# Thirty-two more bytes in two small tiles: starts of the large SBUF tiles in a decoder trunk

## The chip, the cores and the metric

The kernel runs on one core of one Trainium2 chip. The metric is the device time of one execution in microseconds (us); it is given as the median of the runs. A core has a matrix engine (PE, TensorE) that reads both operands from SBUF and adds into PSUM, a vector engine (DVE), an activation engine (ACT), GpSimd (POOL), a queue engine that issues loads (SP), and DMA engines. SBUF has 128 partitions; a tile takes the same byte range in each, and "start" below is the first byte of that range.

## The reference

A trunk of two layers over 256 tokens of width 2048, all in fp32, for one batch:

```python
for i in range(DEPTH):                       # DEPTH = 2
    h = rmsnorm(x, norm_mix[i])
    if i < N_A_LAYERS:                       # layer 0
        x = x + gmlp_mixer(h, ...)           # gelu(h @ w_in), spatial gate, @ w_out
    else:                                    # layer 1
        x = x + nsa_mixer(h, *kvs, ...)      # attention: compressed, selected, window
    x = x + swiglu(rmsnorm(x, norm_ffn[i]), ffn_w_in[i], ffn_w_out[i])   # 2048 -> 5632 -> 2048
    x = ple_add(x, p[i], norm_ple[i], ple_w[i], ple_gate[i])             # gated 2048 x 2048
    if i == N_A_LAYERS - 1:
        kvs = shared_kv(x, ...)              # K/V of three branches, block compression MLP
```

## The kernel before, in words

Every matrix product is made of three matmuls with fp32r operands (`mm3`, lines 101 to 104): each fp32 operand is split into a high and a low part (`split`, lines 92 to 99: ACT copies the high part, DVE subtracts it), and high by high, high by low and low by high are added in PSUM. The activations are the stationary operand (128 columns, loaded by LDWEIGHTS), the weights the moving one, 512 columns wide in most places: the pair of a weight load and a matmul of 512 columns is what the program mainly consists of.

The stages follow each other: the gMLP mixer's `v` and `u` (the input product), its output product `ao`, the FFN of layer 0 (`ffn_unit` makes one 512-column chunk of gate and up in products `p1` to `p7` by a Strassen-like scheme; `fo` is the output product), the gated embedding (`pj`, `pg`), the shared K/V and the attention (`kv`, `ph`, `q`, `s`, `pv`), its output product `bo`, and the FFN and the embedding of layer 1. Weights stream from HBM through `wraw` (line 139, issued on SP) into a tile `raw`, are split into `wh` and `wl`, and are used at once. `weave` (line 178) puts side work between the blocks of a product; nothing in the order depends on the addresses.

Tiles come from pools that lie one behind the other in SBUF in the order in which they are opened. `const` (line 67) holds `ident`, `pk` (gains and other constants, 197 floats a partition, line 77), `neg_half` and the residual stream `x_sb`. `actp` holds the stationary operands: `big_pair` (line 193) makes the pairs hA, hF, hP, hKV, hB under the tag "h" and gT, aT, oT under the tag "big". `tp` holds temporaries (t13 and t24 of the FFN, qh, ql), `sm` small ones (`ssk`, line 640, two buffers of 4 floats), then come the weight pools `w_raw`, `w_wh`, `w_wl` and, in the FFN stages, `w_third` and `exp` with the FFN's extra stationary forms exh and exl (`new_forms`, line 218). In the attention the pools `bp` (KTh, KTl, Vh, Vl) and `at` (pah, pal, pbh, pbl, L) lie there instead. A size is rounded up to 32 bytes, so a tile of 197 floats moves all that lies behind it off a multiple of 512.

Of the kernel before, what the change touches and what calls it, by code (L numbers as in the profile page):

```python
# [9 lines left out]
F32 = mybir.dt.float32  # L10
# [8 lines left out]
P = 128  # L19
# [27 lines left out]
PK_W = PK_ANY + 1  # L47
# [16 lines left out]
def trunk_kernel(ctx: ExitStack, tc: tile.TileContext, a: dict, out: bass.AP):  # L64
    nc = tc.nc

    const = ctx.enter_context(tc.tile_pool(name="const", bufs=1))
    act_p = ctx.enter_context(tc.tile_pool(name="actp", bufs=1))
    tp = ctx.enter_context(tc.tile_pool(name="tp", bufs=2))
    sm = ctx.enter_context(tc.tile_pool(name="sm", bufs=2))  # L70
# [3 lines left out]

    ident = const.tile([P, P], F32, name="ident")
    make_identity(nc, ident)
    pk = const.tile([P, PK_W], F32, name="pk")
    nc.scalar.dma_start(pk, a["pk"])
    neg_half = const.tile([P, 16], F32, name="neg_half")
    nc.vector.memset(neg_half, -0.5)  # L80
    x_sb = const.tile([P, TT, D], F32, name="x_sb")
# [10 lines left out]
    def split(hi, lo, src, scale=None):  # L92

        if scale is None:
            nc.scalar.activation(hi, src, AF.Copy)  # L95
            nc.vector.tensor_tensor(lo, src, f32v(hi), ALU.subtract)  # L96
        else:
            nc.scalar.activation(hi, src, AF.Copy, scale=scale)
            nc.vector.scalar_tensor_tensor(lo, src, scale, f32v(hi), op0=ALU.mult, op1=ALU.subtract)
# [25 lines left out]
    def gen_bank(nm):  # L125
        return ps_gen.tile([P, NC], F32, tag="gen", name=nm)

    def rsqrt_mean(dst, ss, n):

        w = ss.shape[-1]  # L130
        ms = sm.tile([P, 16], F32, tag="ms", name="ms")
        pr = ss.shape[0]
        nc.vector.tensor_scalar(ms[:pr, :w], ss, 1.0 / n, EPS, op0=ALU.mult, op1=ALU.add)
        nc.gpsimd.tensor_tensor(dst, ms[:pr, :w], neg_half[:pr, :w], ALU.pow)
# [409 lines left out]
    with ExitStack() as bctx:  # L544
# [85 lines left out]
        def kv_proc(br, accs):  # L630
            kr = tp.tile([P, TT, G, HD], F32, tag="t0", name="kr")
            for t in range(TT):
                r1 = rs[:, t:t + 1]
                nc.scalar.activation(kr[:, t].rearrange("p g d -> p (g d)"), accs[t][:, :256], AF.Copy, scale=r1)
                split(Vh[:, br, t].rearrange("p g d -> p (g d)"), Vl[:, br, t].rearrange("p g d -> p (g d)"),
                      accs[t][:, 256:], r1)
            sq = tp.tile([P, TT * G, HD], F32, tag="t2", name="sqk")
            krf = kr.rearrange("p t g d -> p (t g) d")
            nc.scalar.activation(sq, krf, AF.Square)
            ssk = sm.tile([P, 4], F32, tag="ssk", name="ssk")  # L640
            nc.vector.tensor_reduce(ssk, sq, axis=AX.X, op=ALU.add)
            rk = sm.tile([P, 4], F32, tag="rk", name="rk")
            rsqrt_mean(rk, ssk, HD)
            nc.vector.tensor_tensor(krf, krf, rk.unsqueeze(2).to_broadcast([P, 4, HD]), ALU.mult)

            def k_T():
                pt = gen_bank("ksT")
                for g in range(G):
                    for t in range(TT):
                        nc.tensor.transpose(pt[:, g * SEQ + t * P:g * SEQ + (t + 1) * P], kr[:, t, g, :], ident)  # L650
                for t in range(TT):
                    bs = slice(16 + t * 256 + br * P, 16 + t * 256 + (br + 1) * P)
                    split(KTh[:, :, bs], KTl[:, :, bs], pt.rearrange("p (g t s) -> p g t s", g=G, t=TT)[:, :, t],
                          pk[:, PK_KN + 1 + br:PK_KN + 2 + br])
            return k_T
# [28 lines left out]

        accs = gemm("kv0", kvT[0], kvT[1], a["kv_w"], CH_D, NC, KD)
        k_T = kv_proc(0, accs)
        hT = big_pair("h", "hB")
        side = [rest, k_T] + [lambda c=c: x_chunk_T(hT, G_MIX1, c) for c in range(NCH)]
        accs = gemm("kv1", kvT[0], kvT[1], a["kv_w"], 2 * CH_D, NC, KD, side)
        k_T = kv_proc(1, accs)  # L690
        accs = gemm("kvc", kvT[0], kvT[1], a["kv_w"], 0, NC, KD, [rest, rest, k_T, rest])
        c_T = cmp_proc(accs)
# [294 lines left out]
```

## Time and profile before

| | us |
|---|---|
| median of three runs | 2329.65 |
| lowest and highest | 2329.06, 2333.55 |
| the profiled execution | 2328.34 |
| its span, from first to last instruction | 2326.6 |

| engine | busy us | share of the span |
|---|---|---|
| PE (matmul) | 2301.5 | 99% |
| PEld (weight loads, beside the matmuls) | 1871.1 | 80% |
| DVE | 1596.1 | 69% |
| ACT | 1170.5 | 50% |
| POOL | 26.6 | 1% |

The rows further down come from one profiled execution. A row of the timeline is one instruction with its start and its duration. Matmuls overlap in the array and their ends are modelled, so the distance between two starts tells the pace, the duration doesn't. In names like `p<-wh,hF0h` the result stands first, then the moving and the stationary operand; buffer numbers are left out.

### The profile page before, as it was taken

The numbers are of one execution on the slowest core, as the hardware profiler recorded it, in microseconds if no ns is written. First come the engines' busy times: TensorE is split into PE (matmuls) and PEld (weight loads), VectorE is DVE, ScalarE is ACT, GpSimd is POOL, SyncE is SP. The second block draws the span as 40 slices with busy tenths as digits, with TensorE's granted clock in tenths as the row PEclk, the third lists the DMA queues.
The fourth block names the chain that finished last, engine by engine and source line by source line (L and its number), as shares of the span: only waits on it lengthen the run. The fifth ranks groups of instructions, "written<-read, shape, count | busy, mean of one in ns | idle before, by whom it ended". The sixth has DMA issues, their size and how long they took to land.

```text
span 2326.6 us, 26376 instructions
## 1 busy us (share of the span) xinstructions
PE 2301.5 (99%) x10419; PEld 1871.1 (80%) x10419; DVE 1596.1 (69%) x1783; ACT 1170.5 (50%) x1335; POOL 26.6 (1%) x26
## 2 busy tenths in 40 slices
PE   8999999999999999999999999999999999999999
PEld 6887788888888888877787987888888888888887
DVE  5565588855887478655567776688747886588544
ACT  6554455533554345445457665555434554355443
POOL 0000000000000000000000000000000000000000
PEclk9999999999999999999999999999999999999999
DMA  8665655565555555555557444455555455455553
GB/s 293 186 188 192 216 215 199 181 206 180 193 199 199 186 193 179 201 186 175 170 177 228 118 143 145 163 199 199 199 182 198 173 207 199 164 207 200 184 191 127
DMA packets 117720, 438.53 MB, mean 188 GB/s; under 512 B 8555, under 2 KB 10731, under 8 KB 117084
## 3 DMA queue, kind: packets, MB, share of 16 engines
q1 hardware_dynamic: 116220, 434.38, 54.1%
q10 hardware_dynamic: 1296, 2.20, 0.3%
q8 instruction: 82, 1.34, 0.2%
q0 software_dynamic: 80, 0.26, 0.0%
q14 instruction: 42, 0.34, 0.0%
HBM read 434.68 MB, written 6.46 MB: 190 GB/s over the span
## 4 chain that ended last, share of the span: by engine, by line
PE 94%; DVE 2%; DMA 2%; ACT 1%; issue 1%; POOL 0%; SPq 0%; DVEq 0%; ACTq 0%
PE p L103 13%; PE p L104 13%; PE p L102 13%; PE fo L102 7%; PE fo L104 7%; PE fo L103 7%; PE pg L104 3%; PE pg L102 3%; PE pg L103 3%; PE ao L103 1%; PE u L102 1%; PE u L104 1%; PE u L103 1%; PE ao L104 1%; PE ao L102 1%; PE bo L103 1%
## 5 line engine op out<-in xcount | busy, mean ns | idle before, releaser
L96 DVE TENSOR_TENSOR wl<-raw,wh 128x2048 fp32r<-128x2048 f32 (+4 forms) x486 | 891.0, 1841 | 575.5 <-ACT wh L95 574.7
L95 ACT ACTIVATE wh<-raw 128x2048 fp32r<-128x2048 f32 (+4 forms) x486 | 754.8, 1555 | 779.8 <-PE fo L104 275.5
L95 ACT ACTIVATE wh<-t 128x1024 fp32r<-128x1024 f32 x132 | 134.6, 1054 | 168.4 <-PE p L104 118.4
L103 PE MATMUL p<-wl,hF1h 128*128 128x512 f32 x462 | 183.5, 397 | 0.0
L103 PE MATMUL p<-wl,hF0h 128*128 128x512 f32 x462 | 183.5, 397 | 0.0
L102 PE MATMUL p<-wh,hF1h 128*128 128x512 f32 x462 | 182.6, 395 | 0.0
L102 PE MATMUL p<-wh,hF0h 128*128 128x512 f32 x462 | 182.6, 395 | 0.0
L104 PE MATMUL p<-wh,hF1l 128*128 128x512 f32 x462 | 182.6, 395 | 0.0
L104 PE MATMUL p<-wh,hF0l 128*128 128x512 f32 x462 | 182.6, 395 | 0.0
L96 DVE TENSOR_TENSOR wl<-t,wh 128x1024 fp32r<-128x1024 f32 x132 | 157.1, 1221 | 15.7 <-ACT wh L95 13.8
L104 PE MATMUL p<-wh,exl 128*128 128x512 f32 x418 | 164.4, 393 | 0.0
L103 PE MATMUL p<-wl,exh 128*128 128x512 f32 x418 | 164.1, 393 | 0.0
L102 PE MATMUL p<-wh,exh 128*128 128x512 f32 x418 | 163.6, 391 | 0.0
L104 PEld LDWEIGHTS p<-wh,hF1l 128*128 128x128 f32 x462 | 86.8, 188 | 20.5
L102 PEld LDWEIGHTS p<-wh,hF1h 128*128 128x128 f32 x462 | 86.8, 188 | 20.6
L104 PEld LDWEIGHTS p<-wh,hF0l 128*128 128x128 f32 x462 | 86.8, 188 | 20.5
L102 PEld LDWEIGHTS p<-wh,hF0h 128*128 128x128 f32 x462 | 86.8, 188 | 20.6
L103 PEld LDWEIGHTS p<-wl,hF1h 128*128 128x128 f32 x462 | 86.8, 188 | 20.3
L103 PEld LDWEIGHTS p<-wl,hF0h 128*128 128x128 f32 x462 | 86.8, 188 | 20.3
L102 PE MATMUL fo<-wh,aT_0h 128*128 128x512 f32 x256 | 101.1, 395 | 0.0
L102 PE MATMUL fo<-wh,aT_1h 128*128 128x512 f32 x256 | 101.1, 395 | 0.0
L103 PE MATMUL fo<-wl,aT_0h 128*128 128x512 f32 x256 | 100.9, 394 | 0.0
(288 smaller groups left out, 4402.3 us busy)
## 6 DMA issues: line engine op xcount, KB each, us to landing
raw<-in_ffn_w_in SPq DMA_DIRECT2D x176, 1024.0 KB, 4.9
raw<-in_ffn_w_out SPq DMA_DIRECT2D x88, 1024.0 KB, 4.9
raw<-in_a_w_in SPq DMA_DIRECT2D x64, 512.0 KB, 3.8
raw<-in_ple_gate SPq DMA_DIRECT2D x32, 1024.0 KB, 4.9
raw<-in_a_w_out SPq DMA_DIRECT2D x16, 1024.0 KB, 4.9
raw<-in_kv_w SPq DMA_DIRECT2D x24, 512.0 KB, 4.0
raw<-in_b_w_out SPq DMA_DIRECT2D x10, 1024.0 KB, 4.9
raw<-in_b_w_in SPq DMA_DIRECT2D x24, 384.0 KB, 3.4
```

The costliest lines, as they stand in the source:

```text
L95: nc.scalar.activation(hi, src, AF.Copy)
L96: nc.vector.tensor_tensor(lo, src, f32v(hi), ALU.subtract)
L102: nc.tensor.matmul(ps, lh, rh, start=start, stop=False)
L103: nc.tensor.matmul(ps, lh, rl, start=False, stop=False)
L104: nc.tensor.matmul(ps, ll, rh, start=False, stop=stop)
```

## The change

Two small tiles get 32 bytes more a partition each: `pk` is allocated with 205 floats instead of 197 (the load fills the first 197), and the two buffers of `ssk` with 12 floats instead of 4 (the first 4 are used).

```diff
     ident = const.tile([P, P], F32, name="ident")
     make_identity(nc, ident)
-    pk = const.tile([P, PK_W], F32, name="pk")
-    nc.scalar.dma_start(pk, a["pk"])
+
+    pk = const.tile([P, PK_W + 8], F32, name="pk")
+    nc.scalar.dma_start(pk[:, :PK_W], a["pk"])
...
-            ssk = sm.tile([P, 4], F32, tag="ssk", name="ssk")
+            ssk = sm.tile([P, 12], F32, tag="ssk", name="ssk")[:, :4]
```

The built programs have the same instructions in the same order with the same waits on every engine. They differ in starts. This is what lies where, in bytes from the start of a partition, and in brackets the remainder by 512:

| tiles | before | after |
|---|---|---|
| x_sb | 17888 (480) | 17920 (0) |
| hA, hF, hP, hKV, hB, high part (`actp`) | 34272 (480) | 34304 (0) |
| gT, aT, oT, high part (`actp`) | 67040 (480) | 67072 (0) |
| t13, t24, qh, ql and others (`tp`) | 99808 to 120288 (480) | 99840 to 120320 (0) |
| raw, wh, wl (FFN stages) | 127904 to 193440 (416) | 128000 to 193536 (0) |
| exh, exl | 201632, 211360 (416) | 201728, 211456 (0) |
| T of the compression MLP (slices of 240 bytes) | 67040, 83424 (480) | 67072, 83456 (0) |
| KTh, KTl | 177056 (416), 181280 (32) | 177152 (0), 181376 (128) |
| Vh, Vl | 185504, 189600 (160) | 185600, 189696 (256) |
| L, two buffers | 203584 (320), 206784 (448) | 203680 (416), 206880 (32) |
| pbh, pbl, pah, pal | 210176 to 224512 (256) | 210272 to 224608 (352) |

The slices that a matmul reads start at whole multiples of 512 bytes into hA to hP, gT to oT, ex, wh and wl where a block is 512 or 384 columns wide, so the remainder holds for them as well.

## Rows read from the trace of the kernel before

**Rows 1.** The page: span, busy time by engine, the chain that ended last.

```profile
span 2326.6 us, 26376 instructions
PE 2301.5 (99%) x10419; PEld 1871.1 (80%) x10419; DVE 1596.1 (69%) x1783; ACT 1170.5 (50%) x1335; POOL 26.6 (1%) x26
...
PE 94%; DVE 2%; DMA 2%; ACT 1%; issue 1%; POOL 0%; SPq 0%; DVEq 0%; ACTq 0%
```

**Rows 2.** Stretches: us, then PE, PEld, DVE, ACT, POOL busy, PEclk, DMA share, GB/s.

```profile
389.62:433.03 43.41, 43.41 (x193) 35.20 (x192) 37.45 (x35) 22.89 (x20) 0.00 (x0) 1.00 0.54 194
500.00:600.00 100.00, 100.00 (x431) 80.37 (x430) 58.34 (x40) 41.05 (x26) 0.00 (x0) 1.00 0.52 181
1371.00:1446.00 75.00, 70.18 (x349) 57.22 (x349) 46.95 (x100) 40.92 (x93) 1.64 (x1) 0.95 0.37 129
```

**Rows 3.** Timeline of PE, FFN output stage: start us, us, engine, line, operation, shapes.

```profile
539.94 0.39 PE L102 MATMUL fo<-wh,aT_0h 128*128 128x512 f32 x1
...
546.94 0.39 PE L102 MATMUL fo<-wh,aT_0h 128*128 128x512 f32 x1
```

**Rows 4.** Timeline of PE at the end of attention.

```profile
1430.30 0.63 PE L103 MATMUL bo<-wl,oTh 128*128 128x512 f32 x1
...
1431.58 0.61 PE L104 MATMUL bo<-wh,oTl 128*128 128x512 f32 x1
```

**Rows 5.** ACT and DVE by shape: count, busy us, mean ns, idle before.

```profile
L95 ACT ACTIVATE wh<-raw 128x1024 fp32r<-128x1024 f32 x132 | 138.6, 1058 | 132.3 <-PE u L104 31.5 <-PE v L104 24.9 <-PE pg L104 22.2
L95 ACT ACTIVATE wh<-t 128x1024 fp32r<-128x1024 f32 x132 | 134.6, 1054 | 168.4 <-PE p L104 118.4 <-DVE t L445 47.2 <-DVE t L442 2.9
...
L95 ACT ACTIVATE pah<-pa 128x512 fp32r<-128x512 f32 x16 | 9.4, 586 | 5.4 <-PE pa L751 5.4
...
L95 ACT ACTIVATE aT_0h<-mT 128x512 fp32r<-128x512 f32 x16 | 8.5, 584 | 0.0
L96 DVE TENSOR_TENSOR wl<-raw,wh 128x1024 fp32r<-128x1024 f32 x132 | 160.8, 1223 | 119.7 <-ACT wh L95 119.3
L96 DVE TENSOR_TENSOR wl<-t,wh 128x1024 fp32r<-128x1024 f32 x132 | 157.1, 1221 | 15.7 <-ACT wh L95 13.8
```

**Rows 6.** Timeline of PE in an FFN unit: nine matmuls on ex tiles.

```profile
364.13 0.39 PE L102 MATMUL p<-wh,exh 128*128 128x512 f32 x1
...
365.52 0.39 PE L102 MATMUL p<-wh,exh 128*128 128x512 f32 x1
...
366.20 0.40 PE L102 MATMUL p<-wh,hF0h 128*128 128x512 f32 x1
366.44 0.39 PE L103 MATMUL p<-wl,hF0h 128*128 128x512 f32 x1
```

**Rows 7.** PE by shape: count, busy us, mean ns.

```profile
L103 PE MATMUL p<-wl,hF1h 128*128 128x512 f32 x462 | 183.5, 397 | 0.0
...
L104 PE MATMUL p<-wh,hF0l 128*128 128x512 f32 x462 | 182.6, 395 | 0.0
L104 PE MATMUL p<-wh,exl 128*128 128x512 f32 x418 | 164.4, 393 | 0.0
...
L102 PE MATMUL p<-wh,exh 128*128 128x512 f32 x418 | 163.6, 391 | 0.0
```

**Rows 8.** Timeline of PE in attention: 512 columns after 256, and values.

```profile
1250.22 0.61 PE L102 MATMUL q<-wh,hBh 128*128 128x512 f32 x2
1250.67 0.40 PE L103 MATMUL q<-wl,hBh 128*128 128x512 f32 x1
...
1284.33 0.28 PE L103 MATMUL pv<-pbl,Vh 128*128 128x256 f32 x1
...
1284.93 0.27 PE L751 MATMUL pa<-ident,L 128*128 128x128 f32 x1
```

**Rows 9.** Timeline of PE in the compression MLP: sixteen matmuls on T.

```profile
1223.89 0.28 PE L576 MATMUL ph<-wh,T 128*128 128x256 f32 x1
...
1225.78 0.35 PE L102 MATMUL q<-wh,hBh 128*128 128x432 f32 x1
```

## The prediction

> **What bounds the kernel now.** I read the page first: TensorE is busy over 99% of the span, and the chain of work that ended last lies on it for 94%; DVE has 2%, DMA 2%, ACT 1% [rows 1]. So anything this change does to copies, loads or activations can touch about 5% of 2326.6 us, and a change of the matmuls' own pace touches nearly all of it. Second, the windows by stretch: in one FFN unit (389.62 to 433.03) PE is busy all 43.41 us while DVE works 37.45 (86%), ACT 22.89, and in the FFN's output stage PE is busy 100 of 100 us and DVE 58 [rows 2]. PE sets the pace there, and the others have room of at least 14%.
>
> Third, the timeline of PE, read from start to start, since the ends of pipelined matmuls are modelled. In the FFN's output stage 30 matmuls of 512 columns start between 539.94 and 546.94 us: 233.3 ns each, at a granted clock of 1.00 [rows 2, 3], which is the 2.4 GHz level. 512 columns at one a cycle would be 213.3 ns. In the stretch whose granted clock averages 0.95 [rows 2] the same matmuls start 0.427 us apart, three in 1.28 [rows 4], and 512 columns at 1.2 GHz are 427 ns: there nothing is added to the columns. So 20 ns of each 233 do not belong to the array's column rate. They belong to something that feeds it, and that is where an address could matter.
>
> **Part 1: what the change removes, adds, moves.** No instruction is added or removed and none changes place on any engine; the copy of `pk` moves the same 197 columns. Only starts in SBUF move. By the built programs `const` and `actp` and `tp` tiles go from 480 to 0 (counted within 512 bytes) and the weight tiles raw, wh, wl and the ex tiles from 416 to 0; the attention's tiles do not reach multiples of 512 (pah, pal, pbh, pbl go from 256 to 352). So the words of the change hold for the operands of the large matmuls, not for the attention.
>
> **Part 2: DVE, ACT, DMA.** Before the change the same operation already stands on different starts. ACT's 128x1024 copy takes 1058 ns from raw (416 to 416) and 1054 ns from t13/t24 (480 to 416); DVE's subtraction behind it 1223 and 1221 ns; ACT's 128x512 from PSUM takes 586 ns into pah (256) and 584 into aT (480) [rows 5]. Three starts, 0.4% apart: I cost these at nothing. All of it lies beside PE anyway, and if it came to 0.4% of the chain's DVE and ACT 3%, it would be 0.3 us. For loads the trace has no second start: a partition gets 4096 bytes in a row, and a start off 512 can touch at most one more piece of 512, an eighth; of DMA's 2% of the chain (46 us) that is an estimated 6 us either way at most. With no row that shows any of it I take zero.
>
> **Part 3: the matmuls.** In the kernel before, the moving operand of a large matmul (wh, wl) starts at 416 and the stationary one (hA, hF, aT, gT, oT, hP, hKV, all in `actp`) at 480: 64 bytes apart. There is one exception, the FFN's ex tiles: stationary at 416, as the moving ones. And these are faster. In a run of nine of them the starts go from 364.13 to 366.20, 230 ns each, and the last three, 365.52 to 366.20, take 0.68 us, 226.7 each; the next operand from hF at 366.20 falls back to the old pace [rows 6]. By group the same is seen in the modelled durations: 391 and 393 ns for ex, 395 and 397 for hF of the same shape [rows 7]. The first six of the nine take 1.39 us, 232 each: the pace falls by and by, so short runs show only part of it. A second sight of the same floor: after 256-column matmuls two of 512 columns start at 1250.22 and the third start is 1250.67, 225 ns each [rows 8]. So 226 to 227 ns is a pace that PE reaches with these operands, and 233.3 one that it is held at in long runs of 416 against 480. What differs for ex is the start within 512 bytes (equal for both operands), and also the place (above byte 200,000, where the others lie below 100,000); the trace can't part these two. After the change both operands of all these matmuls start at 0, so they are equal as ex's are.
>
> Evidence against: 256-column matmuls show no dependence. Sixteen in a row on T, whose slices step by 240 bytes through eight different starts, take 1.89 us, 118 ns each; those on Vh with a moving operand at 256 start 0.60 us for five, 120 ns [rows 8, 9]. Neither is a long run of one relation at 512 columns, and that is where the loss is, so I let ex decide and keep the doubt as a rival.
>
> The sum: the groups by shape hold 8,969 matmuls of 512 columns, 1,254 of them on ex tiles, 418 in each of three groups [rows 7]. 141 of the others start after a wait or another kind and are left out: 7,574 on 416 against 480 at 233.3, and 1,254 on ex at about 230. At 226.5 (between 226.7 and 226) the first gain 6.8 ns, 51.5 us, and the second 3.5 ns, 4.4 us (in longer runs of one relation they would stay at their last pace). Some 2 us of the 56 fall in stretches in which PE waits anyway: 1371 to 1446, for one, has 4.8 of 75 us idle [rows 2]. 54 us are left. Is the room there? The FFN unit's 43.41 us would be about 42.3 with DVE at 37.45, 89%, so nothing else becomes late; and the loads keep the DMA engines busy for 0.52 to 0.54 of these stretches [rows 2]. The profiled execution's own 2328.34 us becomes 2274; the median of the runs shown, 2329.65, becomes 2275. I say 2274.
>
> The spread of this: pace between 225 and 228 ns gives 2262 to 2287.
>
> One rule speaks against all this. The Trainium skill, "SBUF — State Buffer", section "Who interferes with whom", gives TensorE two SBUF read ports, one for the moving operand and one for the weight load, independent of each other, and says that PE never waits on anyone; by it the relation of two starts is worth nothing, and the time stays at 2330. The ex rows [rows 6] speak against it, the 256-column rows [rows 9] for it.
>
> **Rivals.** *No change.* The ex tiles are faster for their place or for the work around them, not for their start, and 233.3 stays. For it: the flat 256-column rows, and that DVE, ACT and DMA are indifferent. Against: no row with 480 against 416 holds 227 over a run, and none of the tiles' other traits has a reason in the trace. The time is 2329.65 within 0.2% (4.7 us, about what a measurement here can tell from no change): 2325 to 2334.
>
> *Deeper.* If equal starts are half of the loss and the straddling of a 512-byte line the other half, aligned tiles go below what ex shows, towards the 213.3 ns of the columns; halfway, 220 ns, the sum is 8,828 times 12.8 ns (from the mean of 232.8 over both kinds), 113 us: 2217. For it: at the lower clock nothing is added to the columns [rows 4]. Against: the 225 to 227 of [rows 6, 8] look like a floor. The Trainium skill, "TensorE: Matmul & The Clock Gate", section "Back-to-back issue gap", gives N/2.4 + 2.5 ns, 215.7 for 512 columns; by that alone it would be an estimated 2179, and the trace disagrees before the change by 17.1 ns a matmul.
>
> *Slower.* Weight load and moving stream now begin at the same byte of a 512-byte row, always, and if two readers of one row get in each other's way, each matmul pays. It decides from 0.5 ns per matmul (4.7 us over 8,969). The upper bound is the largest single step among the rows at that pace, 0.24 us from 366.20 to 366.44 [rows 6]: 6.7 ns more, 59 us; half of it, an estimate, gives 2359. Against: ex has equal starts too and is faster.
>
> *In between.* Only part of the stages gains, as ex does in short runs (230 instead of 226.5): about 3 ns on 8,828, 27 us, 2303.
>
> **How the numbers follow.** The pace of 226.5: 0.40, 2274. In between: 0.08. Deeper: 0.11. No change: 0.30. Slower: 0.11. That is faster 0.59, same 0.30, slower 0.11. The range of 8 in 10 goes from 2225 (the upper half of the deeper case) to 2335 (the end of no change); it leaves out the slower case and about half of the deeper one. For the likeliest case alone it is 2262 to 2287.
>
> **What would show it.** In the profile after, the 30 matmuls of the output stage should take 6.8 us instead of 7.00, an FFN unit 42.3 instead of 43.41, and the ex and hF groups should have the same duration. If the pace is 233.3 still, the start is not the cause. If hF and ex differ as before, it is the place. If the start-to-start times fall and the span doesn't, another engine took over, and the idle time before PE names it. DVE and ACT durations should be within 0.5% of [rows 5]; if they moved, part 2 was wrong.

## The result, and the profile after

| | before | after |
|---|---|---|
| median, us | 2329.36 | 2277.57 |
| lowest and highest | 2326.11, 2333.55 | 2275.97, 2278.04 |
| span of the profiled execution | 2326.6 | 2275.6 |

The ratio of the times is 0.9775, with an interval of 0.9759 to 0.9792. The line of the copy of `pk` is one lower in the changed kernel, so L104 of [rows 7] is L105 here.

The page of the changed kernel: span, busy time by engine, and the chain that ended last.

```profile
span 2275.6 us, 26376 instructions
...
PE 2250.2 (99%) x10419; PEld 1873.7 (82%) x10419; DVE 1592.9 (70%) x1783; ACT 1170.0 (51%) x1335; POOL 26.6 (1%) x26
...
PE 94%; DVE 2%; DMA 2%; ACT 1%; issue 1%; POOL 0%; SPq 0%; DVEq 0%; ACTq 0%
```

PE's busy time fell by 51.3 us and the span by 51.0; PEld, DVE and ACT have the busy time that they had, within 0.2%, and the chain's shares are those of [rows 1]. So nothing came late in place of PE: the work is the same, and PE goes through it faster. The timeline of PE in the FFN's output stage, to be laid beside [rows 3], with 30 matmuls between the two starts:

```profile
523.01 0.39 PE L103 MATMUL fo<-wh,aT_0h 128*128 128x512 f32 x1
...
529.81 0.39 PE L103 MATMUL fo<-wh,aT_0h 128*128 128x512 f32 x1
```

6.80 us, 226.7 ns each, where it was 233.3. And the nine matmuls on ex tiles of [rows 6], with three on hF behind them:

```profile
355.77 0.39 PE L103 MATMUL p<-wh,exh 128*128 128x512 f32 x1
...
357.13 0.39 PE L103 MATMUL p<-wh,exh 128*128 128x512 f32 x1
...
357.81 0.39 PE L103 MATMUL p<-wh,hF0h 128*128 128x512 f32 x1
...
358.49 0.39 PE L103 MATMUL p<-wh,hF0h 128*128 128x512 f32 x1
```

The first six take 1.36 us (226.7 each), the last three 0.68 (226.7), and the three on hF 0.68 as well. The uneven first matmuls of an ex run are gone, and so is the step back up after it. Uneven they were, and not falling by and by: as means over the runs on ex before, the first seven steps from start to start are 229.7, 231.4, 230.1, 235.2, 229.2, 232.0 and 230.8 ns, and only the eighth and ninth are 226.6 and 226.7. After, all nine are 226.6 or 226.7. By shape (count, busy us, mean ns) the same product on hF and on ex now differs by 2 ns (391, 389), where [rows 7] have 395 and 397 for hF against 391 and 393 for ex:

```profile
L104 PE MATMUL p<-wl,hF1h 128*128 128x512 f32 x462 | 180.4, 391 | 0.0
...
L104 PE MATMUL p<-wl,exh 128*128 128x512 f32 x418 | 162.6, 389 | 0.0
```

One FFN unit (stretch, us, then PE, PEld, DVE, ACT and POOL busy, clock, DMA share, GB/s) takes 42.38 us instead of the 43.41 of [rows 2]:

```profile
380.64:423.02 42.38, 42.38 (x194) 35.19 (x192) 37.31 (x36) 22.90 (x20) 0.00 (x0) 1.00 0.55 198
```

What was expected to stay, stayed. ACT and DVE, by shape, beside [rows 5]:

```profile
L96 ACT ACTIVATE wh<-raw 128x1024 fp32r<-128x1024 f32 x132 | 138.7, 1059 | 123.7 <-PE u L105 29.7 <-PE v L105 23.6 <-PE pg L105 21.2
L96 ACT ACTIVATE wh<-t 128x1024 fp32r<-128x1024 f32 x132 | 134.7, 1056 | 166.0 <-PE p L105 133.2 <-DVE t L446 30.0 <-DVE t L443 2.9
...
L96 ACT ACTIVATE pah<-pa 128x512 fp32r<-128x512 f32 x16 | 9.4, 587 | 5.2 <-PE pa L752 5.2
...
L97 DVE TENSOR_TENSOR wl<-raw,wh 128x1024 fp32r<-128x1024 f32 x132 | 160.8, 1222 | 110.6 <-ACT wh L96 110.1
```

And two stretches of PE's timeline: the sixteen 256-column matmuls of the compression MLP, beside [rows 9] (first and last start, fifteen steps), and four of 512 columns in the stretch at a lower granted clock, beside [rows 4].

```profile
1182.76 0.28 PE L577 MATMUL ph<-wh,T 128*128 128x256 f32 x1
...
1184.53 0.28 PE L578 MATMUL ph<-wl,T 128*128 128x256 f32 x1
...
1400.40 0.63 PE L104 MATMUL bo<-wl,oTh 128*128 128x512 f32 x1
...
1401.68 0.63 PE L105 MATMUL bo<-wh,oTl 128*128 128x512 f32 x1
```

118 ns for 256 columns, and 427 ns for 512 at a granted clock of 0.50, the 1.2 GHz level, both as before. The gain lies in matmuls of 512 columns at the 2.4 GHz level: over all of them that another matmul directly follows (8,828 before, 8,821 after) the mean distance between starts went from 232.9 to 226.9 ns, and 6.0 ns on some 8,825 matmuls, about 53 us, cover the 51.0 that the span lost. The 384-column ones stayed at 175 (175.2 and 175.1).

### The profile page after: what moved, and what is told of

Read it like the earlier page. It is cut to its first block, busy times and chain, and to the rows that moved or that the text cites. A ratio compares the mean times of both kernels' runs of the same rounds, so it can differ in the third digit from the quotient of the medians.

```text
span 2275.6 us, 26376 instructions
## 1 busy us (share of the span) xinstructions
PE 2250.2 (99%) x10419; PEld 1873.7 (82%) x10419; DVE 1592.9 (70%) x1783; ACT 1170.0 (51%) x1335; POOL 26.6 (1%) x26
## 4 chain that ended last, share of the span: by engine, by line
PE 94%; DVE 2%; DMA 2%; ACT 1%; issue 1%; POOL 0%; SPq 0%; DVEq 0%; ACTq 0%
PE p L104 13%; PE p L105 13%; PE p L103 13%; PE fo L103 7%; PE fo L105 7%; PE fo L104 7%; PE pg L105 3%; PE pg L103 3%; PE pg L104 3%; PE ao L104 1%; PE ao L105 1%; PE u L104 1%; PE u L105 1%; PE u L103 1%; PE ao L103 1%; PE bo L104 1%
## 5 line engine op out<-in xcount | busy, mean ns | idle before, releaser
L104 PE MATMUL p<-wl,hF0h 128*128 128x512 f32 x462 | 180.5, 391 | 0.0
L104 PE MATMUL p<-wl,hF1h 128*128 128x512 f32 x462 | 180.4, 391 | 0.0
L105 PE MATMUL p<-wh,hF1l 128*128 128x512 f32 x462 | 179.8, 389 | 0.0
L105 PE MATMUL p<-wh,hF0l 128*128 128x512 f32 x462 | 179.8, 389 | 0.0
L104 PE MATMUL p<-wl,exh 128*128 128x512 f32 x418 | 162.6, 389 | 0.0
L105 PE MATMUL p<-wh,exl 128*128 128x512 f32 x418 | 162.6, 389 | 0.0
L104 PEld LDWEIGHTS p<-wl,hF0h 128*128 128x128 f32 x462 | 86.8, 188 | 18.0 <-DVE wl L97 0.4
L104 PEld LDWEIGHTS p<-wl,hF1h 128*128 128x128 f32 x462 | 86.7, 188 | 17.8
L105 PEld LDWEIGHTS p<-wh,hF0l 128*128 128x128 f32 x462 | 86.8, 188 | 17.7
L105 PEld LDWEIGHTS p<-wh,hF1l 128*128 128x128 f32 x462 | 86.7, 188 | 17.7
L105 PE MATMUL fo<-wh,aT_0l 128*128 128x512 f32 x256 | 99.6, 389 | 0.0
```

The source lines that it names most:

```text
L104: nc.tensor.matmul(ps, lh, rl, start=False, stop=False)
L105: nc.tensor.matmul(ps, ll, rh, start=False, stop=stop)
```

## The experiments

The theory in the prediction was that the difference between the starts of the stationary and the moving operand sets the pace. The rivals were the tiles' own alignment to 512 bytes and the place of the ex tiles. Starts below are counted within 512 bytes; "difference" is the stationary start less the moving one. Every diff is against the kernel before, unless the text says otherwise. The fences show two starts 30 matmuls apart in the FFN's output stage, as above.

### Each pad alone

`pk` alone moves `actp` to 0 and the weights to 448:

```diff
-    pk = const.tile([P, PK_W], F32, name="pk")
-    nc.scalar.dma_start(pk, a["pk"])
+    pk = const.tile([P, PK_W + 8], F32, name="pk")
+    nc.scalar.dma_start(pk[:, :PK_W], a["pk"])
```

> Only the pad of pk: the stationary operands start at 0 within 512 bytes, raw, wh, wl and ex at 448; the two operands stay 64 bytes apart as in the kernel before. If the difference between the two starts sets the pace: 233.3 ns between starts for hF, aT, gT, 226 to 230 for ex, 2329 us. If it is the stationary operand's own start at a multiple of 512: 226.7 ns everywhere but on ex, about 2277 us. If it is the moving operand's own start: 233.3 and 2329 us.

```profile
529.62 0.39 PE L102 MATMUL fo<-wh,aT_0h 128*128 128x512 f32 x1
...
536.62 0.39 PE L102 MATMUL fo<-wh,aT_0h 128*128 128x512 f32 x1
```

7.00 us, 233.3 ns; 2328.37 us, ratio 0.9999 (0.999 to 1.0009). The stationary operands and `x_sb` lie at multiples of 512, and it is worth nothing. `ssk` alone moves the weights to 480, where `actp` already is:

```diff
-            ssk = sm.tile([P, 4], F32, tag="ssk", name="ssk")
+            ssk = sm.tile([P, 12], F32, tag="ssk", name="ssk")[:, :4]
```

> Only the pad of ssk: stationary and moving operands of the large matmuls both start at 480 within 512 bytes, equal, and no large tile lies at a multiple of 512 or of 64. If the difference between the starts sets the pace: 226.7 ns, and 2277 us as the full change. If multiples of 512 (or of 64) do: 233.3 ns and 2329 us.

```profile
530.26 0.39 PE L102 MATMUL fo<-wh,aT_0h 128*128 128x512 f32 x1
...
537.06 0.39 PE L102 MATMUL fo<-wh,aT_0h 128*128 128x512 f32 x1
```

6.80 us, 226.7 ns; 2278.00 us, ratio 0.9783 (0.9766 to 0.9799): the whole gain, with no large tile at a multiple of 512 or even of 64. The weights are 64 bytes from where they were and `actp` has not moved at all, so the place isn't it either. What counts is that both operands start alike. The other half of the change, the pad of `pk`, moves both by the same 32 bytes and is worth nothing.

### How far apart, and by which period

From here on the pad of `pk` stays as in the change, so the stationary operands are at 0, and the weights move, by a wider `ssk` and, for odd multiples of 32, a wider `junk`. Difference 256:

```diff
-            ssk = sm.tile([P, 4], F32, tag="ssk", name="ssk")
+            ssk = sm.tile([P, 44], F32, tag="ssk", name="ssk")[:, :4]
```

> Both pads, ssk wider: stationary operands at 0, raw, wh, wl and ex at 256 within 512. If only an equal start is fast: 233.3 ns on hF, aT, gT, 2329 us, ex below. If only a difference of 64 is slow: 226.7 ns, 2277 us. If multiples of 256 are enough: 226.7 ns too.

```profile
530.19 0.39 PE L102 MATMUL fo<-wh,aT_0h 128*128 128x512 f32 x1
...
536.99 0.39 PE L102 MATMUL fo<-wh,aT_0h 128*128 128x512 f32 x1
```

6.80 us; 2277.15 us as the median of two runs, ratio 0.9781 (0.9761 to 0.98). A difference of 256 is as good as none: 226.7 ns.

Moving operands at 128:

```diff
-            ssk = sm.tile([P, 4], F32, tag="ssk", name="ssk")
+            ssk = sm.tile([P, 28], F32, tag="ssk", name="ssk")[:, :4]
```

> Both pads, ssk wider: stationary operands at 0, raw, wh, wl and ex at 128 within 512: the moving operand is 128 bytes ahead. If only an equal start is fast: 233.3 ns on hF, aT, gT, 2329 us. If only the weight start 64 bytes ahead of the moving one is slow: 226.7 ns, 2277 us.

```profile
529.72 0.39 PE L102 MATMUL fo<-wh,aT_0h 128*128 128x512 f32 x1
...
536.69 0.39 PE L102 MATMUL fo<-wh,aT_0h 128*128 128x512 f32 x1
```

6.97 us, 232.3 ns; 2321.09 us, ratio 0.9972 (0.9959 to 0.9986). Neither "only an equal start is fast", which wanted 233.3, nor "only a weight start 64 ahead is slow", which wanted 226.7, hits it; the second is out. Moving operands at 384:

```diff
-            ssk = sm.tile([P, 4], F32, tag="ssk", name="ssk")
+            ssk = sm.tile([P, 60], F32, tag="ssk", name="ssk")[:, :4]
```

> Stationary operands at 0, raw, wh, wl and ex at 384 within 512: 128 apart the other way round than in the run with 128. If the pace depends on the difference within 256 bytes, this is the same difference as there: 232.5 ns, 2321 us. If it depends on the difference within 512, or on which of the two is ahead, it may be anything from 226.7 to 233.3 ns, 2277 to 2329 us.

```profile
529.61 0.39 PE L102 MATMUL fo<-wh,aT_0h 128*128 128x512 f32 x1
...
536.58 0.40 PE L102 MATMUL fo<-wh,aT_0h 128*128 128x512 f32 x1
```

The same 6.97 us; 2321.32 us, ratio 0.9962 (0.9948 to 0.9976). So 128 and 384 are one case, as 0 and 256 are: the pace depends on the difference within 256 bytes. The period was tried at these two places alone; for the other steps below it is taken over from them. Moving operands at 64, 64 ahead of the stationary ones:

```diff
-            ssk = sm.tile([P, 4], F32, tag="ssk", name="ssk")
+            ssk = sm.tile([P, 20], F32, tag="ssk", name="ssk")[:, :4]
```

> Stationary operands at 0, the moving ones at 64: as far apart as in the kernel before, with the moving one ahead. If only the distance counts: 233.3 ns, 2329 us. If a weight load behind the moving stream is harmless and one ahead of it is not: 226.7 ns, 2277 us; with 232.5 at 128 the first is likelier.

```profile
529.79 0.39 PE L102 MATMUL fo<-wh,aT_0h 128*128 128x512 f32 x1
...
536.65 0.39 PE L102 MATMUL fo<-wh,aT_0h 128*128 128x512 f32 x1
```

6.86 us, 228.7 ns; 2294.43 us as the median of two runs, ratio 0.9857 (0.9828 to 0.9885). The sign matters: 64 bytes one way cost 6.6 ns, the other way 2.0. Both expectations missed. Moving operands at 32 and at 480; the diff is against the changed kernel and stands at three places:

```diff
-            junk = sm.tile([P, NC], F32, tag="junk", name="junk", bufs=1)
+            junk = sm.tile([P, NC + 8], F32, tag="junk", name="junk", bufs=1)[:, :NC]
```

For 480 `ssk` also gets 68 floats.

> Stationary operands at 0, the moving ones at 32. If the unit of the difference is 64 bytes: 226.7 ns, 2277 us, or that of a difference of 64, 233.3 and 2329. If every difference costs in proportion up to 64: near 230 ns, 2303 us.

```profile
529.68 0.40 PE L102 MATMUL fo<-wh,aT_0h 128*128 128x512 f32 x1
...
536.69 0.40 PE L102 MATMUL fo<-wh,aT_0h 128*128 128x512 f32 x1
```

> Stationary operands at 0, the moving ones at 480: the stationary start is 32 bytes ahead. If the unit is 64 bytes: 226.7 ns (2277 us) or 233.3 (2329 us). In proportion: near 230 ns, 2303 us. The sign matters if this differs from the run with the moving ones at 32.

```profile
529.79 0.40 PE L102 MATMUL fo<-wh,aT_0h 128*128 128x512 f32 x1
...
536.79 0.40 PE L102 MATMUL fo<-wh,aT_0h 128*128 128x512 f32 x1
```

7.01 and 7.00 us; 2328.61 us, ratio 0.9992 (0.9981 to 1.0003), and 2325.77, ratio 0.9984 (0.9973 to 0.9996). 32 bytes off, either way, cost all of it, so the cost is not in proportion to the difference. Two were left, 160 (`ssk` of 20 floats and the wider `junk`, moving at 96) and 96 (`ssk` of 28 and the wider `junk`, moving at 160). The line of `ssk` for the first, against the changed kernel:

```diff
-            ssk = sm.tile([P, 12], F32, tag="ssk", name="ssk")[:, :4]
+            ssk = sm.tile([P, 20], F32, tag="ssk", name="ssk")[:, :4]
```

> Stationary operands at 0, the moving ones and ex at 96 within 512. So far, by the difference of stationary and moving start within 256: 226.7 ns at 0, 233.3 at 32, 233.3 at 64, 232.4 at 128, 228.9 at 192, 233.3 at 224. This one is 160. If the pace improves from 64 over 128 to 192: between 229 and 232 ns, 2295 to 2320 us. If only whole multiples of 64 are better than 233.3, as 32 and 224 suggest: 233.3 ns, 2329 us.

```profile
530.23 0.39 PE L102 MATMUL fo<-wh,aT_0h 128*128 128x512 f32 x1
...
537.23 0.39 PE L102 MATMUL fo<-wh,aT_0h 128*128 128x512 f32 x1
```

> Stationary operands at 0, the moving ones and ex at 160: a difference of 96 within 256. On either theory of the run with 160 it should be near 233.3 ns and 2329 us; a pace under 226.7 would be a better place for the weights than the change's.

```profile
530.19 0.40 PE L102 MATMUL fo<-wh,aT_0h 128*128 128x512 f32 x1
...
537.22 0.39 PE L102 MATMUL fo<-wh,aT_0h 128*128 128x512 f32 x1
```

7.00 us, 2330.61 us, ratio 1.0004 (0.9993 to 1.0016); and 7.03 us, 234.3 ns, 2334.09 us, ratio 1.0017 (1.0006 to 1.0028), the slowest of all. Together, for the eight steps of 32 within 256, as means over all matmuls on aT of layer 0:

| difference within 256 | 0 | 32 | 64 | 96 | 128 | 160 | 192 | 224 |
|---|---|---|---|---|---|---|---|---|
| ns from start to start | 226.7 | 233.3 | 233.3 | 234.3 | 232.5 | 233.4 | 228.9 | 233.3 |
| us of the kernel | 2277 | 2326 | 2329 | 2334 | 2321 | 2331 | 2294 | 2329 |

There is one best place, and the change is on it. The times follow the paces at 7.3 to 8.1 us for a nanosecond, which is about what the 7,715 matmuls of 512 columns that are not on ex give (the ex tiles move with the weights and keep a difference of 0).

One rival was in none of the expectations: ACT, DVE and the loads write tiles that lie beside the operands or are operands later, so PE could be held up by those writes. The traces before and after rule it out. In the kernel before, the 206 steps on aT around which neither ACT nor DVE nor POOL works take 233.4 ns, and the 1,701 around which one of them works most of the time 233.3; the 505 around which no DMA moves anything and the 1,569 others take 233.3 as well. After, every one of these groups stands at 226.7. So the loss lies within PE and its own operand streams.

The scan also shows what before and after hide: the 384-column matmuls (of `q`) do depend on the starts, but by another rule. They take 175.2 ns at a difference of 64 and 175.1 at 0, but 173.2 at 192 and 176.5 at 160 (one run each), where three runs at 0 agree within 0.7 ns, two at 64 within 0.4 and two at 128 within 0.1. Zero isn't their best place.

### One of three loads

The low parts of the stationary operands are put at 64, and all else is as in the changed kernel, against which this diff of `big_pair` is:

```diff
-        hi = act_p.tile([P, KD, SEQ], F32R, tag=tag + "h", name=nm + "h")
-        lo = act_p.tile([P, KD, SEQ], F32R, tag=tag + "l", name=nm + "l")
-        return hi, lo
+        hi = act_p.tile([P, KD * SEQ + 16], F32R, tag=tag + "h", name=nm + "h")
+        lo = act_p.tile([P, KD * SEQ + 112], F32R, tag=tag + "l", name=nm + "l")
+        return tuple(x[:, :KD * SEQ].rearrange("p (k s) -> p k s", s=SEQ) for x in (hi, lo))
```

> As the full change, but the low parts of the stationary operands (hAl, hFl, aTl, gTl, oTl, hPl, hKVl, hBl) start at 64 within 512, the high parts and the moving operands at 0. One matmul of three then has the difference of the kernel before. If each such weight load costs its own 6.7 ns: 228.9 ns on average over hF and aT, some 2292 us. If a single one is absorbed, as the first matmuls of a run were: 226.7 ns and 2277 us. If one of three is enough to hold all: 233.3 ns, near 2325 us.

The timeline of PE in the output stage:

```profile
539.96 0.40 PE L104 MATMUL fo<-wh,aT_0l 128*128 128x512 f32 x1
540.19 0.39 PE L102 MATMUL fo<-wh,aT_0h 128*128 128x512 f32 x1
540.42 0.39 PE L103 MATMUL fo<-wl,aT_0h 128*128 128x512 f32 x1
540.65 0.40 PE L104 MATMUL fo<-wh,aT_0l 128*128 128x512 f32 x1
540.89 0.39 PE L102 MATMUL fo<-wh,aT_0h 128*128 128x512 f32 x1
```

2308.20 us as the median of two runs, ratio 0.9899 (0.987 to 0.9928). Three matmuls take 0.69 to 0.70 us, 231.1 ns each over the stage; the step after a start on the low part is the long one (0.23 to 0.24 us in these rows, 236 ns as a mean over 342 of them, against 228 and 229 for the other two). One load of three at the bad difference costs 13 ns of the 20 that three cost. None of the three expectations hits that: the load neither costs just its own 6.7 ns, nor is it absorbed, nor does it hold back all three.

The last run asks which pair of addresses meets: a matmul's own two operands, or the streaming operand and the weights loaded meanwhile for the next one. Against the run before, the low parts' pads change to 48 floats, and wl starts 64 bytes into its tile:

```diff
+        if nm == "wl":
+            return pool.tile([P, cur["kt"] * NC + 64], dt, tag=nm, name=nm)[:, 16:16 + cur["kt"] * NC]
         return pool.tile([P, cur["kt"] * NC], dt, tag=nm, name=nm)
```

> As the run with the low parts at 64, and wl too is sliced 64 bytes into its (wider) tile. Now a matmul and its own stationary operand differ by 0, 192 and 64 (within 256) in the three matmuls of a product, but the weights that are loaded while a matmul streams, those of the next one, always differ by 0 from what it streams. If the next load against the running stream counts: 226.7 ns and 2277 us, as the full change. If a matmul's own two operands count: 231 ns or more, 2308 us or more, as the run before had it with one of three at 64.

```profile
530.04 0.40 PE L102 MATMUL fo<-wh,aT_0h 128*128 128x512 f32 x1
...
536.97 0.40 PE L102 MATMUL fo<-wh,aT_0h 128*128 128x512 f32 x1
```

6.93 us, 231.0 ns; 2312.99 us, ratio 0.993 (0.9914 to 0.9947). The theory of the next load wanted 226.7 and falls. The theory of the own operands said 231 or more and stands on these tiles, but not on ex: there the moving and the stationary start within 256 are 0 and 0 for the first of the three matmuls, 64 and 0 for the second and 0 and 0 for the third, so the differences are 0, 192 and 0. The nine matmuls on ex between these two starts

```profile
363.00 0.40 PE L102 MATMUL p<-wh,exh 128*128 128x512 f32 x1
...
365.09 0.39 PE L102 MATMUL p<-wh,hF0h 128*128 128x512 f32 x1
```

take 2.09 us, 232 ns each, where two at 226.7 and one at 228.9 would be 227.4. Nor is it left over from the hF run in front, as the first steps on ex were before: in the runs of nine the last three steps still take 229.2, 233.4 and 235.0 ns as means over 66 such runs, where in the kernel before they take 230.8, 226.6 and 226.7. Something beside a matmul's own two starts counts. What sets this run's tiles apart is that the moving start changes from one matmul to the next, but no run has that alone. Which two reads meet, and where, stays open.

## Why the prediction was right

**The bound and the room** (first part, part 2): right. PE carried the change alone; ACT's and DVE's durations moved by 2 ns at most against [rows 5], and the FFN unit has DVE at 37.31 of 42.38 us, 88%, where 89% was worked out.

**The floor of 226 to 227 ns, read from nine ex matmuls and two after 256-column ones** [rows 6, 8]: right by the first and lucky in the second. At a difference of 0 the steady pace is 226.7 ns, the value of the last three of the nine. The two after 256-column ones were no sight of it: they stand on hB and wh, 64 bytes apart, and are the first of a run, where steps scatter. The same two take 232 and 231 ns after the change, and over all 21 such starts before, the first step is 230.2 ns. At most they moved the forecast pace from 226.7 to 226.5. Nor did the pace on ex fall by and by, as the prediction read from one run; it scatters for seven steps and then stands. The reason that it gave for ex, equal starts within 512 bytes, was right in kind (the run with `ssk` alone) and too narrow: the period is 256. The place as the rival is out by the same run.

**The terms of the sum.** On all but ex 6.8 ns were forecast and 6.3 measured (233.3 to 226.95; in the long runs on aT it is 6.6), so 51.5 us were some 48; on ex 3.5 ns were forecast, from 230 to 226.5, and 3.9 measured, since ex before averaged 230.6 over all its runs, so 4.4 us were 4.9. The 2 us taken off for stretches in which PE waits were about right: the two terms make about 53 us, and the span lost 51.0. Forecast in all 54, measured 52 between the medians. The stated range of 2225 to 2335 could not have told this from no change; the sum, and its own 2262 to 2287, could.

**What the prediction left out.** It said that after the change both operands "are equal as ex's are" without asking how near equal is near enough. The scan shows that 32 bytes either way would have given next to nothing. And its flat 256-column rows on T, named as evidence against, are flat after as well [rows 9]: those matmuls show no part in it. Those on Vh are no test, since their difference is 160 in both kernels.

**The rivals.** No change: its mechanism (the place) is refuted. Deeper: no run's mean went below 226.7 ns; the run at 480 and 480, off every multiple of 64, has the same floor as the one at 0 and 0, so straddled lines are no second half. Slower: equal starts are the best of the eight, but a place worse than the kernel before exists, at a difference of 96, with 1 ns and 0.17%. In between: short runs reach the same pace as long ones, all nine steps on ex standing at 226.6 or 226.7 after. The rule of the Trainium skill, "SBUF — State Buffer", "Who interferes with whom", that TensorE's two read ports are independent and PE never waits on anyone, doesn't hold here as a rule of time: the two runs that have the same instructions, with one small tile wider in each, stand at 233.3 and 226.7 ns.

## What to carry to other kernels

When fp32r matmuls of 512 columns run back to back, work out from the allocation where the stationary and the moving operand start, and bring their difference to a multiple of 256 bytes. Here one padded small tile between the two pools did it, and neither operand needed to be aligned to 512. Nearly equal is not enough: 32 bytes off cost nearly all of the gain. Keep the high and low parts of a split operand on the same start as well, since one load of three off it cost two thirds of the loss. Before that, look for it in the trace: compare start-to-start of two groups of the same shape that differ in nothing but their tiles, over many steps, since the first seven or so of a run and single steps scatter. Other widths, and other types, have to be tried by themselves.

## What the runs showed of the hardware that was not expected

- At a granted clock of 1.00 a matmul of 512 fp32r columns with a weight load each keeps 226.7 ns at best and 233 to 234 at worst, by the difference of the two operands' starts within 256 bytes; at the 1.2 GHz level it is 427 ns, 512 columns at that clock, before and after.
- The dependence is not monotonic: 0 and 192 are good (226.7, 228.9), 128 a little better than the rest (232.5), the odd multiples of 32 all bad (233.3 to 234.3).
- Such a pace can be the mean of a repeating pattern: at a difference of 192 the steps on aT go 226, 229, 232 ns over and over, at 160 232, 238, 230, while at 0 nearly every step is 226 or 227.
- Matmuls of 256 columns on T show nothing of it (118 ns before and after); those of 384 move between 173.2 and 176.5 ns over the scan, and not with the 512-column ones.
- ACT and DVE show nothing of it: 1058 and 1059 ns, 1223 and 1222 ns for the same copy and subtraction. Nor do the 1 MB weight loads of the FFN, which land after 4.9 to 5.0 us in every run.
